# A decoder trunk kernel: the rotation's cosine product stays in PSUM, its sine halves and doubled keys are one operation each, and two softmax row tiles share one reciprocal

## The chip, the cores and the metric

The kernel runs on one core of a Trainium2 chip. The metric is the device time of one execution, in microseconds (us). The core's engines work side by side, each through its own queue of instructions in order: PE (TensorE, matrix products and transposes; its weight loads are shown as PEld), DVE (VectorE), ACT (ScalarE), POOL (GpSimd) and SP (which issues the DMAs). Semaphores hold an instruction back until what it needs is there. SBUF is the working memory, PSUM the memory into which PE writes, in banks of 512 f32 columns.

## The reference, cut to what matters

Two layers over 512 tokens of width 1024. Each layer is a mixer of three attention groups and then a gated MLP with a short convolution, both with norms before and after.

```
proj = h @ w_in                                  # one projection, cut into q, k, v of three head groups
rope(x): x1, x2 = x[..., :8], x[..., 8:16]       # HEAD_DIM 64, of which 16 are rotated
    concat([x1*cos - x2*sin, x2*cos + x1*sin, x[..., 16:]])
o_fox = fox_attention(q, k, v, log_f)            # 4 heads, not rotated
o_nsa = nsa_attention(rope(nq), rope(kc), vc, rope(ks), vs, rope(kw), vw, gates, ...)   # 8 heads, 2 key groups
o_dil = dilated_attention(rope(dq), rope(dk), dv)                                       # 4 heads
masked_softmax(s): e = exp(s - max(s)); e / sum(e)
x = x + rms_norm(concat(o_fox, o_nsa, o_dil) @ w_out)
x = x + rms_norm(conv_ffn(rms_norm(x)))
```

## The kernel before

**Numbers.** A matrix operand is held as a high part and a low part (hi and lo, `wh`/`wl`, `ph`/`pl`), and a product is three matmuls (hi·hi, hi·lo, lo·hi). For each such operand ACT copies the high part and DVE or POOL subtracts it from the original to get the low part. So every evacuation of PSUM and every arriving weight costs one ACT and one DVE or POOL operation.

**Attention stage.** `units` is a list of 96 softmax row tiles per layer: for each head (and for each of two branches in the nsa group) four tiles t = 0 to 3 of 128 queries, with 128·(t+1) keys. A loop runs over slots; in each slot every unit that is under way takes one step: scores (PE), `st_max` (DVE: mask and row minimum, since scores are negated), `st_exp` (ACT, with the row sum), `st_norm` (a reciprocal of the sum on DVE, then POOL scales the row, line 1133), `st_turn` (PE transposes, line 1146), `st_keep_hi` (ACT, line 1157) and `st_keep_lo` (DVE, line 1162), values (PE), `st_out`. `LAGS` says how many slots after its scores a unit takes each step: norm two slots, transposes four. The transposes of t = 0 are made together with those of t = 1.

**Between the units** the loop sprinkles pieces of the projections (`main_pieces`): `kc`, `ks`, `nq0`, `kw`, `nq1`, `dv`, `dq`, `dk`. A projection makes four token tiles s = 0 to 3 of 256 columns; tiles 0 and 1 lie in one PSUM bank, 2 and 3 in the next. Each tile is evacuated by `rope`: a cosine product `t1` (line 468) and two sine products into halves of `t2` (lines 469 and 470), all read from PSUM and written to SBUF tiles named `rope`; then for each destination an addition (line 472, `r<-rope,rope`) and an ACT copy of the 48 columns that are not rotated (line 473). Keys (`ks`, `kw`, `dk`) are stored twice side by side, so they have two destinations. Four token tiles are then transposed (line 737) and split into `k` or `q` (lines 493 and 486). In the same stretch the compressed branch builds windows `wt` (line 795), half on DVE, half on POOL.

**Order.** PE's order is written out by hand; the order on DVE, ACT and POOL is set by a scheduler that plans all instructions beforehand, and each engine then goes through its list.

Of the kernel before, what the change touches and what calls it, by code (L numbers as in the profile page):

```python
# [9 lines left out]
F32 = mybir.dt.float32  # L10
F32R = mybir.dt.float32r
I32 = mybir.dt.int32
AF = mybir.ActivationFunctionType
ALU = mybir.AluOpType
# [60 lines left out]
def tile_hybrid_block(  # L75
# [6 lines left out]
    nc = tc.nc  # L82
# [6 lines left out]
    small = ctx.enter_context(tc.tile_pool(name="small", bufs=8))  # L89
# [5 lines left out]
    def nm(p):  # L95
        uid[0] += 1
        return f"{p}_{uid[0]}"
# [7 lines left out]
    def rt(shape=(128, 512), dt=F32):  # L105
        return rowp.tile(list(shape), dt, tag="r", name=nm("r"))

    def st(n, tag="sm"):
        return small.tile([128, n], F32, tag=tag, name=nm("sm"))
# [7 lines left out]
    def bc(ap, axis, n):  # L117
        a = ap.unsqueeze(axis)
        shape = list(a.shape)
        shape[axis] = n  # L120
        return a.to_broadcast(shape)
# [318 lines left out]
    cc = const.tile([128, NST, 16], F32, name="cc")  # L440
    ss = const.tile([128, NST, 16], F32, name="ss")
# [6 lines left out]
    for l in range(DEPTH):  # L448
# [14 lines left out]
                mm(o, HL(k)[:, sl], w[0][:, i], False, last and z == n - 1)  # L463

        def rope(dst, src, s, nh):
            t1 = small.tile([128, nh, 16], F32, tag="rope", bufs=4, name=nm("rope"))
            t2 = small.tile([128, nh, 16], F32, tag="rope", bufs=4, name=nm("rope"))
            nc.vector.tensor_mul(t1, src[:, :, 0:16], bc(cc[:, s], 1, nh))
            nc.vector.tensor_mul(t2[:, :, 0:8], src[:, :, 8:16], bc(ss[:, s, 0:8], 1, nh))
            nc.vector.tensor_mul(t2[:, :, 8:16], src[:, :, 0:8], bc(ss[:, s, 8:16], 1, nh))  # L470
            for d in dst:
                nc.vector.tensor_add(d[:, :, 0:16], t1, t2)  # L472
                nc.scalar.activation(d[:, :, 16:64], src[:, :, 16:64], AF.Copy)

        def t_block(tiles, c0):
            p = ps("pt")
# [27 lines left out]
        def hd(ap):  # L504
            return ap.rearrange("p (h d) -> p h d", d=64)
# [5 lines left out]
        bias = small.tile([128, 28], F32, tag="gbias", bufs=1, name=nm("gbias"))  # L511
# [9 lines left out]
        for s in range(NST):  # L521
# [5 lines left out]
            p = ps("s")[:, 0:284]  # L527
# [6 lines left out]
            d = rt((128, 4, 2, 64))  # L534
# [7 lines left out]
        for j in range(3):  # L542
            d = crow[44 * (j % 2):44 * (j % 2) + 44, j // 2, :]
# [170 lines left out]
        def staged(key, turned, dup, nh, v=None, plain=0):  # L714

            tl = []

            def evac(s, p):
                w = nh * 64 * (2 if dup else 1)
                d = rt((128, w + plain))  # L720
                if dup:
                    e = d[:, 0:w].rearrange("p (h u d) -> p h u d", h=nh, u=2)
                    rope([e[:, :, 0, :], e[:, :, 1, :]], hd(p[:, 0:64 * nh]), s, nh)
                else:
                    rope([hd(d[:, 0:w])], hd(p[:, 0:64 * nh]), s, nh)
                if plain:
                    nc.scalar.activation(d[:, w:w + plain], p[:, 64 * nh:64 * nh + plain], AF.Copy)
                if v is not None:
                    if s == 0:
                        store[v] = new_v()  # L730
                    v_evac(store[v], s, p[:, 64 * nh:64 * nh + 128])
                tl.append(d)

            def turn(j):
                p = ps(TT)
                for s in range(NST):
                    nc.tensor.transpose(p[:, 128 * s:128 * s + 128], tl[s][:, 128 * j:128 * j + 128], ident)  # L737
                pieces.later(EV[3], keep, p)

            def keep(p):  # L740
                store.setdefault(key, []).append((k_evac if dup else q_evac)(p))

            return evac, [(turn, j) for j in range(nh * (2 if dup else 1) // 2)]
# [6 lines left out]
        def main_pieces():  # L750
# [2 lines left out]

            def kc_evac(s, p):
                d = rt((128, 256))
                rope([hd(d[:, 0:128])], hd(p[:, 0:128]), s, 2)
                nc.scalar.activation(d[:, 128:256], p[:, 128:256], AF.Copy)
                tl.append(d)

# [356 lines left out]

        def st_max(u):
            n = u["n"]
            row, sm_ = rt(), st(3, "sf")
            u["row"], u["sm"] = row, sm_  # L1120
            nc.vector.tensor_tensor_reduce(row[:, 0:n], u["S"][:, 0:n], u["mask"][:, 512 - n:512], op0=ALU.add,  # L1121
                                           op1=ALU.min, scale=1.0, scalar=3.0e38, accum_out=sm_[:, 0:1])

        def st_exp(u):
            n, row, sm_ = u["n"], u["row"], u["sm"]
            nc.scalar.activation(row[:, 0:n], row[:, 0:n], AF.Exp, scale=-1.0, bias=sm_[:, 0:1],  # L1126
                                 accum_out=sm_[:, 1:2])

        def st_norm(u):
            n, row, sm_ = u["n"], u["row"], u["sm"]  # L1130
            nc.vector.reciprocal(sm_[:, 2:3], sm_[:, 1:2])  # L1131
            g_ = 1.0 if u["gate"] is None else gates[:, u["t"], u["gate"]:u["gate"] + 1]
            nc.gpsimd.tensor_scalar(row[:, 0:n], row[:, 0:n], sm_[:, 2:3], g_, op0=ALU.mult, op1=ALU.mult)  # L1133

        def st_turn(u):
            if u["t"] == 0:
# [276 lines left out]
```

## Time and profile before

| what | value |
|---|---|
| time, median of 3 runs (lowest to highest) | 1375.59 us (1375.48 to 1377.04) |
| the profiled execution: its own time, and its span from first to last instruction | 1373.89 us, 1372.1 us |
| PE busy | 1337.1 us, 97% |
| DVE busy | 865.5 us, 63% |
| ACT busy | 730.7 us, 53% |
| POOL busy | 287.4 us, 21% |
| granted TensorE clock, share of full | 0.998 |

The first layer's attention stage lies at about 50 to 350 us of the span, its MLP at 350 to 690; the second layer's at 720 to 1030 and after. Busy shares over the whole span are means over these stages. In the views, `A<-B` names the tile written and the tiles read, `L472` is line 472 of the kernel, and "idle before <-X" says which instruction ended an engine's wait.

### The profile page before, as it was taken

The numbers are of one execution on the slowest core, as the hardware profiler recorded it, in microseconds if no ns is written. First come the engines' busy times: TensorE is split into PE (matmuls) and PEld (weight loads), VectorE is DVE, ScalarE is ACT, GpSimd is POOL, SyncE is SP. The second block draws the span as 40 slices with busy tenths as digits, with TensorE's granted clock in tenths as the row PEclk, the third lists the DMA queues.
The fourth block names the chain that finished last, engine by engine and source line by source line (L and its number), as shares of the span: only waits on it lengthen the run. The fifth ranks groups of instructions, "written<-read, shape, count | busy, mean of one in ns | idle before, by whom it ended". The sixth has DMA issues, their size and how long they took to land.

```text
span 1372.1 us, 21230 instructions
## 1 busy us (share of the span) xinstructions
PE 1337.1 (97%) x7855; PEld 1176.5 (86%) x7855; DVE 865.5 (63%) x2021; ACT 730.7 (53%) x1530; POOL 287.4 (21%) x343
## 2 busy tenths in 40 slices
PE   9999999999999999999999999999999999999997
PEld 8899998978888888888898899999798888888886
DVE  7688877778655555433464887877876555554334
ACT  6567767777533333333465677677774333333232
POOL 1364753341000000000004546633210000000000
PEclk9999999999999999999999999999999999999999
DMA  6323311141333333323333142012323333332231
GB/s 180 93 63 110 100 43 48 47 138 32 108 93 97 102 92 96 104 93 123 111 97 91 48 138 78 32 47 63 123 62 93 104 96 92 99 101 92 94 122 62
DMA packets 145520, 123.76 MB, mean 90 GB/s; under 512 B 8264, under 2 KB 135688, under 8 KB 145416
## 3 DMA queue, kind: packets, MB, share of 16 engines
q1 hardware_dynamic: 145416, 122.40, 29.4%
q8 instruction: 62, 1.02, 0.3%
q14 instruction: 42, 0.34, 0.1%
HBM read 118.19 MB, written 4.19 MB: 89 GB/s over the span
## 4 chain that ended last, share of the span: by engine, by line
PE 81%; DVE 10%; ACT 5%; issue 2%; POOL 1%; DMA 0%; SPq 0%; ACTq 0%; DVEq 0%
PE acc L115 36%; PE s L115 18%; PE pt L115 12%; PE o L115 10%; PE pt L1146 3%; DVE r L472 1%; DVE wt L795 1%; DVE hl L271 1%; DVE r L1121 1%; DVE pl L1162 1%; ACT r L1126 1%; PE pt L737 1%; ACT hh L270 1%; ACT r L1195 0%; ACT ph L1157 0%
## 5 line engine op out<-in xcount | busy, mean ns | idle before, releaser
L154 DVE TENSOR_TENSOR wl_up<-raw_up,wh_up 128x1024 fp32r<-128x1024 f32 x78 | 95.6, 1226 | 170.8 <-ACT wh_up L146 170.8
L146 ACT ACTIVATE wh_up<-raw_up 128x1024 fp32r<-128x1024 f32 (+1 forms) x90 | 89.6, 1001 | 160.4 <-PE acc L115 68.1
L154 DVE TENSOR_TENSOR wl_wd<-raw_wd,wh_wd 128x1024 fp32r<-128x1024 f32 x42 | 51.5, 1226 | 133.7 <-ACT wh_wd L146 133.7
L146 ACT ACTIVATE wh_wd<-raw_wd 128x1024 fp32r<-128x1024 f32 x42 | 44.5, 1060 | 144.8 <-PE pt L115 135.5
L1126 ACT ACTIVATE r<-r,sm 128x128 f32<-128x128 f32 x192 | 106.7, 557 | 22.1 <-DVE sm L1121 20.5
L1133 POOL TENSOR_SCALAR r<-r,sm,gates 128x128 f32<-128x128 f32 (+3 forms) x128 | 86.4, 680 | 117.0 <-DVE sm L1131 80.5
L115 PE MATMUL acc<-hl,wh_up 128*128 128x512 f32 (+1 forms) x272 | 102.4, 377 | 0.0
L115 PE MATMUL acc<-hh,wh_up 128*128 128x512 f32 (+1 forms) x272 | 102.4, 377 | 0.0
L115 PE MATMUL acc<-hh,wl_up 128*128 128x512 f32 (+1 forms) x272 | 102.4, 377 | 0.0
L150 POOL TENSOR_TENSOR wl_kc<-raw_kc,wh_kc 128x512 fp32r<-128x512 f32 x8 | 11.8, 1489 | 417.6 <-ACT wh_kc L146 416.7
L115 PE MATMUL s<-k,q 128*128 128x512 f32 (+3 forms) x384 | 96.4, 337 | 2.8 <-DVE sm L1121 1.3
L1162 DVE TENSOR_TENSOR pl<-pt,ph 128x384 fp32r<-128x384 f32 x144 | 85.5, 595 | 13.4 <-ACT ph L1157 11.6
L1121 DVE CUSTOM_DVE_ANT_0 r<-s,cmask 128x128 f32<-128x128 f32 (+3 forms) x160 | 75.8, 483 | 18.9 <-PE s L115 13.5
L1157 ACT ACTIVATE ph<-pt 128x384 fp32r<-128x384 f32 x144 | 75.5, 524 | 21.6 <-PE pt L1146 20.0
L1146 PE MATMUL pt<-ident,r 128*128 128x128 f32 x480 | 77.2, 275 | 7.2 <-DVE pl L1162 5.7
L115 PE MATMUL acc<-wh_wd,gh 128*128 128x512 f32 x252 | 83.7, 389 | 0.0
L115 PE MATMUL s<-hh,wh_up 128*128 128x512 f32 (+1 forms) x224 | 80.4, 359 | 0.0
L115 PE MATMUL s<-hl,wh_up 128*128 128x512 f32 (+1 forms) x224 | 80.4, 359 | 0.0
L115 PE MATMUL s<-hh,wl_up 128*128 128x512 f32 (+1 forms) x224 | 80.4, 359 | 0.0
L1337 ACT ACTIVATE r<-r 128x512 f32<-128x512 f32 x44 | 27.8, 633 | 85.7 <-DVE r L1318 85.5
L1146 PEld LDWEIGHTS pt<-ident,r 128*128 128x128 f32 x480 | 55.2, 140 | 16.2 <-POOL r L1133 7.1
L115 PE MATMUL acc<-wh_wo,mix 128*128 128x256 f32 (+1 forms) x296 | 67.6, 305 | 0.0
(440 smaller groups left out, 4145.6 us busy)
## 6 DMA issues: line engine op xcount, KB each, us to landing
raw_up<-in_w_up_dram SPq DMA_DIRECT2D x88, 512.0 KB, 3.8
raw_wd<-in_w_down_dram SPq DMA_DIRECT2D x44, 512.0 KB, 3.4
raw_wo<-in_w_out_dram SPq DMA_DIRECT2D x16, 512.0 KB, 3.5
x<-in_x_dram SPq DMA_DIRECT2D x8, 512.0 KB, 5.9
raw_nq<-in_w_in_dram SPq DMA_DIRECT2D x8, 512.0 KB, 3.5
raw_w<-in_cmp_w_k_dram SPq DMA_DIRECT2D x8, 512.0 KB, 3.9
raw_w<-in_cmp_w_v_dram SPq DMA_DIRECT2D x8, 512.0 KB, 3.8
raw_fk<-in_w_in_dram SPq DMA_DIRECT2D x4, 512.0 KB, 5.6
```

The source lines that it names most:

```text
L115: nc.tensor.matmul(o, lhsT=lhsT, rhs=rhs, start=start, stop=stop, skip_group_check=True)
L146: nc.scalar.activation(hi[:, ks], raw[:, ks], AF.Copy)
L154: nc.vector.tensor_sub(lo[:, ks], raw[:, ks], f(hi)[:, ks])
L270: nc.scalar.activation(hi, src, AF.Copy, scale=gain[:, k:k + 1])
L271: nc.vector.scalar_tensor_tensor(lo, src, gain[:, k:k + 1], f(hi), op0=ALU.mult, op1=ALU.subtract)
L1121: nc.vector.tensor_tensor_reduce(row[:, 0:n], u["S"][:, 0:n], u["mask"][:, 512 - n:512], op0=ALU.add, op1=ALU.min, scale=1.0, scalar=3.0e3 ...
L1126: nc.scalar.activation(row[:, 0:n], row[:, 0:n], AF.Exp, scale=-1.0, bias=sm_[:, 0:1], accum_out=sm_[:, 1:2])
L1133: nc.gpsimd.tensor_scalar(row[:, 0:n], row[:, 0:n], sm_[:, 2:3], g_, op0=ALU.mult, op1=ALU.mult)
L1146: nc.tensor.transpose(p[:, 128 * c:128 * c + 128], blocks[z], ident)
L1157: nc.scalar.activation(hi, src, AF.Copy)
L1162: nc.vector.tensor_sub(*u["lo"])
L1337: nc.scalar.activation(cd[0], cd[0], AF.Silu)
```

## The change

`rope` now takes one destination with a dimension u for the copies. It makes `t2` in one operation, reading the two halves of the rotated columns in swapped order (a step of -8). The cosine product is written over the 16 columns in PSUM from which it is read. One addition, with `t1` from PSUM and `t2` from SBUF, both broadcast over u, writes all copies; one ACT copy does the same for the other 48 columns. In the softmax, the row sums of t = 0 and t = 1 lie in two columns of one small tile; the step of t = 0 only remembers its unit, and the step of t = 1 makes one reciprocal of both columns and then has POOL scale both rows. t = 2 and t = 3 keep their own reciprocals.

```diff
         def rope(dst, src, s, nh):
-            t1 = small.tile([128, nh, 16], F32, tag="rope", bufs=4, name=nm("rope"))
+
+            t1 = src[:, :, 0:16]
             t2 = small.tile([128, nh, 16], F32, tag="rope", bufs=4, name=nm("rope"))
-            nc.vector.tensor_mul(t1, src[:, :, 0:16], bc(cc[:, s], 1, nh))
-            nc.vector.tensor_mul(t2[:, :, 0:8], src[:, :, 8:16], bc(ss[:, s, 0:8], 1, nh))
-            nc.vector.tensor_mul(t2[:, :, 8:16], src[:, :, 0:8], bc(ss[:, s, 8:16], 1, nh))
-            for d in dst:
-                nc.vector.tensor_add(d[:, :, 0:16], t1, t2)
-                nc.scalar.activation(d[:, :, 16:64], src[:, :, 16:64], AF.Copy)
+            z = src[:, :, 8:16]
+            swapped = bass.AP(tensor=z.tensor, offset=z.offset, ap=[list(z.ap[0]), list(z.ap[1]), [-8, 2], [1, 8]])
+            nc.vector.tensor_mul(t2.rearrange("p h (i d) -> p h i d", i=2), swapped,
+                                 bc(ss[:, s].rearrange("p (i d) -> p i d", i=2), 1, nh))
+            nc.vector.tensor_mul(t1, t1, bc(cc[:, s], 1, nh))
+
+            nu = dst.shape[2]
+            nc.vector.tensor_add(dst[:, :, :, 0:16], bc(t1, 2, nu), bc(t2, 2, nu))
+            nc.scalar.activation(dst[:, :, :, 16:64], bc(src[:, :, 16:64], 2, nu), AF.Copy)
...
         def st_max(u):
             n = u["n"]
-            row, sm_ = rt(), st(3, "sf")
-            u["row"], u["sm"] = row, sm_
+            t = u["t"]
+            row = u["row"] = rt()
+            if t != 1:
+                state["m"] = st(4 if t == 0 else 2, "sf")
+            n2 = 2 if t < 2 else 1
+            u["sm"] = sm_ = [st(1, "mn")] + [state["m"][:, n2 * i + t % n2:n2 * i + t % n2 + 1] for i in range(2)]
+            u["all"] = [state["m"][:, n2 * i:n2 * i + n2] for i in range(2)]
...
         def st_norm(u):
-            n, row, sm_ = u["n"], u["row"], u["sm"]
-            nc.vector.reciprocal(sm_[:, 2:3], sm_[:, 1:2])
-            g_ = 1.0 if u["gate"] is None else gates[:, u["t"], u["gate"]:u["gate"] + 1]
-            nc.gpsimd.tensor_scalar(row[:, 0:n], row[:, 0:n], sm_[:, 2:3], g_, op0=ALU.mult, op1=ALU.mult)
+
+            if u["t"] == 0:
+                state["u"] = u
+                return
+            nc.vector.reciprocal(u["all"][1], u["all"][0])
+            for z in (state["u"], u) if u["t"] == 1 else (u,):
+                n, row = z["n"], z["row"]
+                g_ = 1.0 if z["gate"] is None else gates[:, z["t"], z["gate"]:z["gate"] + 1]
+                nc.gpsimd.tensor_scalar(row[:, 0:n], row[:, 0:n], z["sm"][2], g_, op0=ALU.mult, op1=ALU.mult)
```

PE and SP go through the same instructions in the same order as before. On the other three engines the scheduler has planned anew.

First place: DVE, in the first layer, where the last two token tiles of the `ks` projection (`acc_961` before, `acc_954` now) are evacuated while the windows `wt` are built; L1121 and L1126 are the row minimum of a softmax tile, L502 and L506 the low part of the values. Before:

```order
L472 TENSOR_TENSOR r_1204<-rope_1205,rope_1206 128x2x16 x2
L1121 ISA r_1221,sm_1222<-s_1140,cmask 128x512
L1121 ISA sm_1222 128x1
L795 TENSOR_TENSOR wt_1201<-r_1199,posT_803 64x16x31
L502 TENSOR_TENSOR v_1137<-acc_961,v_1137 128x2x64
L468 TENSOR_TENSOR rope_1254<-acc_961,cc 128x32
L469 TENSOR_TENSOR rope_1255<-acc_961,ss 128x2x8
L470 TENSOR_TENSOR rope_1255<-acc_961,ss 128x2x8
L795 TENSOR_TENSOR wt_1201<-r_1199,posT_803 64x16x31
L472 TENSOR_TENSOR r_1253<-rope_1254,rope_1255 128x2x16 x2
```

And with the change:

```order
L476 TENSOR_TENSOR r_1191<-acc_954,rope_1192 128x4x16
L1126 ISA r_1204,sm_1206<-s_1129,cmask 128x512
L1126 ISA sm_1206 128x1
L795 TENSOR_TENSOR wt_1188<-r_1186,posT_803 64x16x31
L506 TENSOR_TENSOR v_1126<-acc_954,v_1126 128x2x64
L471 TENSOR_TENSOR rope_1238<-acc_954,ss 128x32
L795 TENSOR_TENSOR wt_1188<-r_1186,posT_803 64x16x31
L473 TENSOR_TENSOR acc_954<-acc_954,cc 128x2x16
L1139 RECIPROCAL sm_1205<-sm_1205 128x1
L476 TENSOR_TENSOR r_1237<-acc_954,rope_1238 128x4x16
```

The sequence around the windows is the same; each pair of additions of two SBUF tiles is one addition with one operand in PSUM, and a reciprocal now stands ahead of the second addition.

Second place: POOL, in the first layer's first two softmax heads (L1133 and L1143 scale a row; L150 is a weight's low part). Before:

```order
L1133 TENSOR_SCALAR r_1017<-r_1017,sm_1018 128x512
L1133 TENSOR_SCALAR r_1044<-r_1044,sm_1045 128x128
L150 TENSOR_TENSOR wl_nq_1_203_1233<-raw_nq_1_170_1075,wh_nq_1_202_1232 128x512
L795 TENSOR_TENSOR wt_1073<-r_1071,posT_803 64x16x31 x2
L150 TENSOR_TENSOR wl_nq_1_203_1233<-raw_nq_1_170_1075,wh_nq_1_202_1232 128x512
L1133 TENSOR_SCALAR r_1103<-r_1103,sm_1104 128x256
```

And with the change:

```order
L1143 TENSOR_SCALAR r_1010<-r_1010,sm_1011 128x512
L150 TENSOR_TENSOR wl_nq_1_202_1217<-raw_nq_1_170_1070,wh_nq_1_201_1216 128x512
L795 TENSOR_TENSOR wt_1068<-r_1066,posT_803 64x16x31 x2
L150 TENSOR_TENSOR wl_nq_1_202_1217<-raw_nq_1_170_1070,wh_nq_1_201_1216 128x512
L1143 TENSOR_SCALAR r_1038<-r_1038,sm_1039 128x128
L1143 TENSOR_SCALAR r_1098<-r_1098,sm_1039 128x256
```

The row of t = 0 (128x128) is scaled just ahead of the row of t = 1 (128x256) and no longer before the weight and window work.

## Rows read from the trace of the kernel before

**Rows 1.** The page, part 1: busy us of each engine (share) and instructions.
```profile
PE 1337.1 (97%) x7855; PEld 1176.5 (86%) x7855; DVE 865.5 (63%) x2021; ACT 730.7 (53%) x1530; POOL 287.4 (21%) x343
```

**Rows 2.** Stretches: attention, then MLP; busy us of each engine, clock, DMA share, GB/s.
```profile
50.00:100.00 50.00, 47.95 (x378) 45.73 (x377) 34.57 (x105) 27.91 (x80) 31.16 (x29) 1.00 0.23 65
400.00:450.00 50.00, 50.00 (x222) 41.40 (x221) 27.54 (x33) 18.70 (x23) 0.00 (x0) 1.00 0.33 95
```

**Rows 3.** PE's waits: us in total, times, longest.
```profile
PE pt L1146 <- DVE pl L1162: 5.7, 6, 1.8
PE pt L737 <- DVE pl L1162: 4.6, 4, 2.2
```

**Rows 4.** PE's timeline where it waits: start, us, what, idle time before it.
```profile
93.00 0.55 PE L737 MATMUL pt<-ident,r 128*128 128x128 f32 x3 [1.45 <-DVE pl L1162]
...
132.49 0.50 PE L115 MATMUL s<-k,q 128*128 128x128 f32 x2 [0.48 <-DVE k L493]
...
765.47 0.44 PE L115 MATMUL s<-k,q 128*128 128x384 f32 x1 [0.68 <-DVE sm L1121]
...
771.43 0.44 PE L737 MATMUL pt<-ident,r 128*128 128x128 f32 x2 [2.17 <-DVE pl L1162]
```

**Rows 5.** DVE's timeline, 84.5 to 93 us.
```profile
84.70 0.16 DVE L469 TENSOR_TENSOR rope<-acc,ss 128x16 f32<-128x16 f32 x1
84.79 0.16 DVE L470 TENSOR_TENSOR rope<-acc,ss 128x16 f32<-128x16 f32 x1
85.05 1.39 DVE L472 TENSOR_TENSOR r<-rope,rope 128x32 f32<-128x32 f32 x2
...
88.95 1.45 DVE L795 TENSOR_TENSOR wt<-r,posT 64x496 f32<-64x496 f32 x1
90.42 1.24 DVE L472 TENSOR_TENSOR r<-rope,rope 128x32 f32<-128x32 f32 x2
```

**Rows 6.** POOL's timeline, same stretch.
```profile
85.11 1.29 POOL L802 TENSOR_TENSOR wth<-wt,wth 128x512 fp32r<-128x512 f32 x1
...
87.73 3.78 POOL L795 TENSOR_TENSOR wt<-r,posT 64x496 f32<-64x496 f32 x2
```

**Rows 7.** The tile `rope`: shortest/median/longest ns, first and last start.
```profile
L472 DVE TENSOR_TENSOR r<-rope,rope x80: 176/215/1331, 64.4 to 913.7; 128x32 f32<-128x32 f32 x40, 128x64 f32<-128x64 f32 x40
L468 DVE TENSOR_TENSOR rope<-acc,cc x56: 169/204/225, 64.0 to 911.3; 128x64 f32<-128x64 f32 x32, 128x32 f32<-128x32 f32 x24
```

**Rows 8.** DVE's groups by shape: count, busy us, mean ns, idle before.
```profile
L1131 DVE RECIPROCAL sm<-sm 128x1 f32<-128x1 f32 x192 | 29.3, 155 | 17.2 <-ACT r L1126 16.5
...
L472 DVE TENSOR_TENSOR r<-rope,rope 128x32 f32<-128x32 f32 x40 | 16.1, 434 | 1.1
...
L472 DVE TENSOR_TENSOR r<-rope,rope 128x64 f32<-128x64 f32 x40 | 12.5, 328 | 0.8
```

**Rows 9.** DVE's timeline in the second layer, same place as rows 5.
```profile
762.25 2.56 DVE L472 TENSOR_TENSOR r<-rope,rope 128x32 f32<-128x32 f32 x2
...
768.87 1.22 DVE L472 TENSOR_TENSOR r<-rope,rope 128x32 f32<-128x32 f32 x2
```

**Rows 10.** Timelines at the `kw` projection, first layer: DVE, then ACT.
```profile
124.07 2.58 DVE L472 TENSOR_TENSOR r<-rope,rope 128x32 f32<-128x32 f32 x2
...
130.57 0.60 ACT L492 ACTIVATE k<-pt 128x512 fp32r<-128x512 f32 x1 [0.40 <-PE pt L737]
```

**Rows 11.** All engines' waits: us in total, times, longest.
```profile
ACT r L473 <- DVE rope L470: 21.8, 18, 2.6
...
PEld pt L1146 <- POOL r L1133: 7.1, 8, 2.0
```

**Rows 12.** What ended DVE's idle time before line 468: us, times.
```profile
  ACT r L473: 0.5, 2
```

**Rows 13.** ACT's and POOL's groups by shape: count, busy us, mean ns, idle before.
```profile
L473 ACT ACTIVATE r<-acc 128x192 f32<-128x192 f32 x40 | 12.2, 326 | 8.3 <-DVE rope L470 5.6 <-PE pt L1146 2.6
...
L1133 POOL TENSOR_SCALAR r<-r,sm,gates 128x128 f32<-128x128 f32 x32 | 15.2, 476 | 24.5 <-DVE sm L1131 19.4 <-PE s L115 3.5 <-DVE rope L468 1.6
```

More of the change, by code (lines that the diff above doesn't have):

```diff
@@ L720, in evac @@
                 d = rt((128, w + plain))
[L721 to L725, printed above, removed]
+                rope(d[:, 0:w].rearrange("p (h u d) -> p h u d", h=nh, d=64), hd(p[:, 0:64 * nh]), s, nh)
                 if plain:
@@ L755, in kc_evac @@
                 d = rt((128, 256))
-                rope([hd(d[:, 0:128])], hd(p[:, 0:128]), s, 2)
+                rope(d[:, 0:128].rearrange("p (h u d) -> p h u d", h=2, d=64), hd(p[:, 0:128]), s, 2)
                 nc.scalar.activation(d[:, 128:256], p[:, 128:256], AF.Copy)
@@ L1118, in st_max @@
             n = u["n"]
-            row, sm_ = rt(), st(3, "sf")
-            u["row"], u["sm"] = row, sm_
+            t = u["t"]
[5 more added lines that the diff above has]
+            u["all"] = [state["m"][:, n2 * i:n2 * i + n2] for i in range(2)]
             nc.vector.tensor_tensor_reduce(row[:, 0:n], u["S"][:, 0:n], u["mask"][:, 512 - n:512], op0=ALU.add,
-                                           op1=ALU.min, scale=1.0, scalar=3.0e38, accum_out=sm_[:, 0:1])
+                                           op1=ALU.min, scale=1.0, scalar=3.0e38, accum_out=sm_[0])
         def st_exp(u):
             n, row, sm_ = u["n"], u["row"], u["sm"]
-            nc.scalar.activation(row[:, 0:n], row[:, 0:n], AF.Exp, scale=-1.0, bias=sm_[:, 0:1],
-                                 accum_out=sm_[:, 1:2])
+            nc.scalar.activation(row[:, 0:n], row[:, 0:n], AF.Exp, scale=-1.0, bias=sm_[0],
+                                 accum_out=sm_[1])
         def st_norm(u):
-            n, row, sm_ = u["n"], u["row"], u["sm"]
-            nc.vector.reciprocal(sm_[:, 2:3], sm_[:, 1:2])
-            g_ = 1.0 if u["gate"] is None else gates[:, u["t"], u["gate"]:u["gate"] + 1]
-            nc.gpsimd.tensor_scalar(row[:, 0:n], row[:, 0:n], sm_[:, 2:3], g_, op0=ALU.mult, op1=ALU.mult)
+            if u["t"] == 0:
[6 more added lines that the diff above has]
+                nc.gpsimd.tensor_scalar(row[:, 0:n], row[:, 0:n], z["sm"][2], g_, op0=ALU.mult, op1=ALU.mult)
         def st_turn(u):
```

## The prediction

> **What bounds the kernel.** I read the busy times first. PE is busy for 1337.1 us of a span of 1372.1, DVE for 63% of it [rows 1]. So 35 us at most are to be had without taking work from PE, and this change takes none. Then the table by stretches: in the MLP PE is busy for all 50.00 of 50 us, in the attention stage for 47.95, with DVE at 34.57 there [rows 2]. Everything that the change touches lies in the attention stages, so its worth is what it does to the few microseconds that PE waits there. Third, PE's waits by releaser: the longest entries are waits for DVE, 5.7 and 4.6 us, both ended by line 1162, the low part of the turned softmax rows [rows 3]. That line is cheap and regular; it is late because of what stands ahead of it in DVE's queue. So last I went to PE's gaps one by one and read DVE's timeline backwards from each.
>
> Four gaps have rotations ahead of them: 1.45 us at 93.00 and, at the same place in the second layer, 0.68 at 765.47 and 2.17 at 771.43; and 0.48 at 132.49 [rows 4], with its twin in the second layer, which I take as equal. In the first, the addition pair at 85.05 takes 1.39 us and the pair at 90.42 takes 1.24 [rows 5], where an addition has a median of 0.215 and reaches 1.331 [rows 7]. POOL's operation at 85.11 ends at 86.40, and the pair ends at 86.44; POOL's two at 87.73 end at 91.51, the pair at 91.66 [rows 5, 6]. So the additions stand still until POOL is through. The cosine product, which reads one operand from PSUM and one from SBUF, never takes over 0.225 in 56 times, though it runs in the same stretches [rows 7]. What tells them apart in these rows is the two SBUF operands of line 472.
>
> **The change part by part.**
>
> *The additions.* Their 80 take 16.1 + 12.5 = 28.6 us [rows 8]; at 0.2 each they would take 16, so 12.6 us are standing still. After the change 56 are left, with one operand in PSUM. No row shows such an addition, nor DVE writing PSUM, which the cosine product now does. The nearest rows are line 468 (0.204) and the free line 472 (0.215) [rows 7]; I take 0.2 for each, and as the other end twice that, which over 112 operations would be 22 us more on DVE.
>
> [...]
>
> *Place A, windows and `ks`.* First layer: the pair at 85.05 becomes one addition of 0.2, so DVE is 1.2 us earlier, and the one at 90.42 is 1.0 earlier by itself. In between stand two window operations with two SBUF operands (1.45 at 88.95 [rows 5]), which also meet POOL, so part of the first 1.2 may be lost there. The gap of 1.45 needs 1.45 of the 2.2: I take 1.3 (bounds 0 and 1.45). Second layer: the pairs take 2.56 and 1.22 [rows 9] and would take 0.25 each, 3.3 us less, against gaps of 0.68 + 2.17 = 2.85; by the same share I take 2.4 (bounds 0.95, if only the last addition counts, and 2.85).
>
> *Place B, `kw`.* The pair at 124.07 takes 2.58 [rows 10] and DVE then works on until the gap at 132.49. 2.3 us earlier is more than the gap needs, but the low part of `k` for which PE waits also needs ACT's copy, 130.57 to 131.17 [rows 10], which itself waits for PE's transposes. 0.45 of 0.48 in each layer, 0.9 (bounds 0 and 0.96).
>
> *Fewer operations.* 48 of 192 reciprocals go, 0.155 each, 7.4 us of DVE [rows 8], and 56 sine products, which in a row cost only 0.09 each (84.70 to 84.79 [rows 5]), 5 us. These lie across both attention stages, where PE is waiting for some 4% of the time [rows 2], so most of it shortens nothing: 0.5 (bounds 0 and 3).
>
> *What it adds to `rope`.* Before, the three products do not depend on each other, and only the addition waits: 84.79 to 85.05, 0.26 [rows 5]. Now the cosine product overwrites columns that the sine product reads, so it waits for that, and the addition waits for it: two steps of 0.27 and 0.2, about 0.75, against 0.1 + 0.09 + 0.26 + 0.2 = 0.65. 0.1 us for each of 56 tiles is 5.6 us of DVE, which cancels the saved sine products. ACT's copy, which already waits for line 470 (21.8 us in 18 waits [rows 11]), now waits for the addition, some 0.4 later; what stands behind it in ACT's queue is a copy of values or a softmax copy. DVE's first product of the next tile in the bank waits for ACT's copy: that wait is there today and costs 0.5 us in two waits [rows 12]. I charge 0.4 (bounds 0 and the rival below).
>
> *Rows of t = 0 scaled later.* POOL scales the row of t = 0 just ahead of that of t = 1, 0.476 [rows 13]. The transposes come two slots after, so there is usually cover; PE's weight loads already wait for POOL 8 times, 7.1 us in all [rows 11]. If each of those became 0.476 longer, it would be 3.8; in the tail of each stage the two stand together already. I charge 0.3 (bounds 0 and 3.8).
>
> **The sum.** 1.3 + 2.4 + 0.9 + 0.5 - 0.4 - 0.3 = 4.4 us. Against the profiled execution's own 1373.89 (span 1372.1 and 1.8 around it) that is 1369.5; that execution was 1.7 below the median of the three timed runs, 1375.59, to which I refer the forecast: 1371.2. A difference under 0.2%, 2.75 us, can hardly be told from none here, so the forecast stands 1.65 us beyond that bound.
>
> **Rivals.**
>
> *The standing still moves on* (15%). The next operation with two SBUF operands meets the POOL operation in place of the addition: at place A the window operations of line 795 stand right behind the first addition. Then only the last addition of the place counts, 0.95 in each layer, and with B, the fewer operations and the costs the gain is 1.9 + 0.9 + 0.5 - 0.7 = 2.6: 1373.0. For it: 1.45 for a window operation beside POOL [rows 5]. Against it: at B the operations behind the pair are rotations and value splits that read PSUM.
>
> [...]
>
> *The serial rotation ends slower* (14%). In 28 of the 56 tiles DVE's sine product waits for ACT's copy of the tile before it in its bank, and everything behind it on DVE, the row minima and line 1162, waits too. If the copy (0.326 for 192 columns [rows 13]), now 0.4 later, is waited for in full at each, that is 28 x 0.73 = 20 us of DVE standing still, more than the 12.6 gained. PE then waits longer at the projections' ends instead of shorter; at a quarter of the surplus and with the gaps of A and B as they were, and the transposes behind POOL's paired rows, I reckon 3 us more than before: 1378.5. It decides from a mean wait of 0.45 us per tile pair (12.6/28). Against it: the scheduler has put other work between most of these pairs, and the waits of today are 0.5 us in all [rows 12].
>
> *The write into PSUM is dear* (8%). At the upper bound, 22 us of DVE eat the 12.6 + 7.4: no change, 1375.3.
>
> *A lighter DVE helps everywhere* (13%). The other gaps behind line 1162 [rows 3] shrink as well, the fewer operations reach their bound of 3, and A and B close fully (1.45 + 2.85 + 0.96 = 5.3): some 8 us, 1367.
>
> **How the numbers follow.** The forecast case has 50% (1368.5 to 1373.2, nine in ten of it beyond the bound). Faster by over 0.2%: 0.45 + 0.13 + a third of the first rival, 0.63. Within 0.2%: 0.05 + 0.10 + 0.08, 0.23. Slower: 0.14. The range leaves out the far ends of the last and of the slower rival: 1366.5 to 1377.0.
>
> **What the profile after would show.** Right: no rotation's addition over 0.3 us, their busy time near 12 us in place of 28.6; PE's gaps at about 93, 132 and 765 to 771 gone or under 0.4; PE's busy time unchanged, its idle time some 4 us less; DVE busy about 30 us less. The first rival would show window operations longer by what the additions lost. The slower one would show DVE waiting for the ACT copy of the rotation by more than 10 us, and PE waiting for DVE at the turns of `q` and `k`. What would make me wrong altogether is a new plan that moves line 1162 behind other work at places where today it is on time, since each such case costs PE 1 to 2 us and I read the order only where the gaps are today.

## The result, and the profile of the changed kernel

The changed kernel takes 1368.51 us (median of 6 executions, 1368.02 to 1369.85) against 1375.61 for the kernel before (6 executions beside them): a ratio of 0.9947, 95% interval 0.9934 to 0.9960. It is 7.1 us faster; the forecast was 4.4. The profiled execution took 1369.85 (span 1367.9) and is the slowest of its six, while that of before was 1.7 under its median; so the two spans differ by 4.2 only, and the rest of this document has to say where the other 3 us lie.

The page's part 1, as [rows 1]:

```profile
PE 1338.0 (98%) x7855; PEld 1177.9 (86%) x7855; DVE 850.4 (62%) x1893; ACT 728.2 (53%) x1506; POOL 287.0 (21%) x343
```

The rotation's lines, as [rows 7, 8] (here over all shapes: busy us, mean ns, idle before). Line 471 is the sine product, 473 the cosine product written into PSUM, 476 the addition; line 1139 is the reciprocal.

```profile
L1139 DVE RECIPROCAL sm<-sm 128x2 f32<-128x2 f32 x144 | 22.7, 158 | 17.6 <-ACT r L1131 17.1
...
L795 DVE TENSOR_TENSOR wt<-r,posT 64x496 f32<-64x496 f32 x8 | 13.9, 1740 | 2.5 <-ACT r L783 2.4
L476 DVE TENSOR_TENSOR r<-acc,rope 128x64 f32<-128x64 f32 (+2 forms) x56 | 12.6, 226 | 1.9
L473 DVE TENSOR_TENSOR acc<-acc,cc 128x64 f32<-128x64 f32 (+1 forms) x56 | 12.0, 215 | 1.4
```

No addition stands still any more: in the view by tile they take 190 to 293 ns. Writing PSUM costs hardly more than writing SBUF did (215 ns a cosine product, 203 before).

PE's timeline at place A in both layers, as [rows 4]:

```profile
92.37 0.66 PE L737 MATMUL pt<-ident,r 128*128 128x128 f32 x4 [0.55 <-DVE pl L1172]
766.99 0.66 PE L737 MATMUL pt<-ident,r 128*128 128x128 f32 x4 [0.55 <-DVE pl L1172]
```

Line 1172 is what line 1162 was. The gap of 1.45 is 0.55, those of 0.68 and 2.17 are one of 0.55, and at place B (0.48 at 132.49) there is none. The stretch of both places, first layer, before and after (busy us of PE, PEld, DVE, ACT, POOL, then clock, DMA share, GB/s):

```profile
60.00:150.00 90.00, 87.77 (x699) 85.20 (x698) 68.91 (x228) 61.43 (x170) 48.66 (x50) 1.00 0.31 89
```

```profile
60.00:150.00 90.00, 89.42 (x712) 86.86 (x711) 65.31 (x197) 61.51 (x165) 49.03 (x51) 1.00 0.31 90
```

PE's idle time there goes from 2.23 to 0.58 us. What is left at A reads in DVE's timeline, as [rows 5]:

```profile
86.53 1.81 DVE L795 TENSOR_TENSOR wt<-r,posT 64x496 f32<-64x496 f32 x1
...
88.66 1.59 DVE L795 TENSOR_TENSOR wt<-r,posT 64x496 f32<-64x496 f32 x1
...
91.42 0.42 DVE L1126 CUSTOM_DVE_ANT_0 r<-s,cmask 128x256 f32<-128x256 f32 x1 [0.51 <-POOL wt L795]
```

Before, the first of the two was (the second is in [rows 5]):

```profile
86.98 1.48 DVE L795 TENSOR_TENSOR wt<-r,posT 64x496 f32<-64x496 f32 x1
```

The window additions, which keep two SBUF operands, now take 1.81 and 1.59 where they took 1.48 and 1.45: some of the standing still has moved on to them. And a row minimum behind them now waits itself.

**The clock.** Elsewhere PE's waits are the same within 0.3 us, with one exception that is not a wait. PE, second layer, in single microseconds (clock is the third number from the end):

```profile
893.00:894.00 1.00, 0.68 (x5) 0.47 (x4) 0.97 (x3) 0.00 (x0) 0.00 (x0) 1.00 0.00 0
894.00:895.00 1.00, 0.80 (x4) 0.83 (x5) 0.61 (x5) 0.91 (x3) 0.20 (x1) 0.51 0.48 143
895.00:896.00 1.00, 1.00 (x7) 1.00 (x6) 0.25 (x1) 0.98 (x5) 1.00 (x1) 0.50 0.82 324
896.00:897.00 1.00, 1.00 (x6) 1.00 (x6) 0.97 (x3) 0.98 (x4) 0.09 (x1) 0.50 0.14 57
897.00:898.00 1.00, 1.00 (x6) 0.98 (x6) 0.79 (x3) 0.20 (x1) 0.80 (x2) 0.79 0.00 0
```

At the last of three gaps (0.47, 0.17 and 0.53 us at 891 to 894) the granted clock falls to 0.50 and stays there for some 3 us, with PE busy from 894.20 on. Matmuls of 256 columns start 0.213 us apart in it (895.08 to 897.22), so PE goes through 1.2 columns a ns; before the gaps, at 1.00, they start 0.12 apart (889.76 to 890.49). The first trace of before has the same three gaps (0.47, 0.18 and 0.52 at 896 to 900) and no such fall. By the table below the fall costs 1.4 us, and the profiled execution is 1.3 above its median; the other five have no trace.

**A table of stretches.** PE's order is the same in every kernel here, so the start of the same matmul can be read from each PE timeline, and the time between two of them compared. us; * marks a stretch in which the trace shows the clock at 0.50 for some 3 us. "55 to 162" holds place A and B of the first layer, "720 to 836" those of the second; the times are those of the changed kernel. The kernels below it are those of the experiments.

| kernel | start to 55 | 55 to 162 | 162 to 217 | 217 to 720 | 720 to 836 | 836 to 891 | 891 to end | median us |
|---|---|---|---|---|---|---|---|---|
| before, [rows 1 to 13] | 54.8 | 108.4 | 55.5 | 504.1 | 118.9 | 55.3 | 475.2 | 1375.6 |
| changed | 55.0 | 106.7 | 55.0 | 504.1 | 115.5 | 54.9 | 476.6* | 1368.51 |
| e1 rotation alone | 55.7 | 106.6 | 56.9* | 504.3 | 115.5 | 56.9* | 476.7* | 1373.62 |
| e2 reciprocal alone | 55.2 | 108.2 | 55.4 | 504.1 | 116.9 | 55.2 | 475.2 | 1375.02 |
| e3 merged, SBUF | 55.0 | 107.2 | 55.1 | 504.1 | 116.0 | 55.1 | 475.2 | 1369.32 |
| e4 PSUM, not merged | 55.0 | 109.0 | 55.6 | 505.9* | 117.9 | 55.6 | 475.5 | 1375.77 |
| e5 before again | 55.8 | 108.4 | 55.4 | 504.1 | 120.0* | 55.4 | 475.2 | 1376.40 |
| e6 as e3, reciprocal shared | 54.6 | 107.3 | 55.1 | 504.1 | 116.1 | 55.2 | 475.2 | 1369.65 |
| e7 sine halves alone | 54.9 | 108.8 | 55.2 | 504.1 | 116.5 | 55.2 | 475.2 | 1372.84 |
| e8 doubled keys alone | 55.8 | 106.7 | 55.1 | 504.1 | 116.6 | 55.2 | 475.2 | 1370.04 |
| e9 as e1, line 950 on ACT | 54.9 | 106.6 | 54.2 | 504.0 | 115.6 | 54.2 | 475.2 | 1366.77 |
| e10 changed, line 952 split | 54.6 | 106.7 | 54.5 | 504.1 | 115.6 | 54.5 | 476.7* | 1367.73 |
| e11 windows on DVE | 54.9 | 110.5 | 54.9 | 505.8* | 120.1* | 54.9 | 475.2 | 1377.90 |
| e12 changed, line 950 on ACT | 54.8 | 106.7 | 54.2 | 504.1 | 115.5 | 54.2 | 475.2 | 1366.73 |

A stretch with a fall is longer than the same one without: by 1.4 and 1.5 us at the end (476.6 and 476.7 against 475.2), by 1.7 and 1.8 at 217 to 720 (505.8 and 505.9 against 504.1), and by 1.1 between the two executions of before (120.0 against 118.9). The start differs by up to 1.2 us between these executions. The traces of e2 and e7 are those of their fastest executions (1371.94 and 1371.54), so their stretches add up to less than their medians. The change itself is worth 1.7 + 0.5 + 3.4 + 0.4 = 6.0 us between the two first rows, most of it in the two stretches with A and B.

### The profile page after: what moved, and what is told of

Read it like the earlier page. It is cut to its first block, busy times and chain, and to the rows that moved or that the text cites. A ratio compares the mean times of both kernels' runs of the same rounds, so it can differ in the third digit from the quotient of the medians.

```text
span 1367.9 us, 21028 instructions
## 1 busy us (share of the span) xinstructions
PE 1338.0 (98%) x7855; PEld 1177.9 (86%) x7855; DVE 850.4 (62%) x1893; ACT 728.2 (53%) x1506; POOL 287.0 (21%) x343
## 4 chain that ended last, share of the span: by engine, by line
PE 85%; DVE 7%; ACT 4%; POOL 2%; issue 2%; DMA 0%; SPq 0%; ACTq 0%; POOLq 0%; DVEq 0%
PE acc L115 39%; PE s L115 19%; PE pt L115 13%; PE o L115 10%; PE pt L1156 3%; POOL wt L795 1%; PE pt L737 1%; DVE hl L271 1%; DVE pl L1172 1%; DVE r L1126 1%; ACT r L1131 1%; DVE x L913 0%; ACT hh L270 0%; ACT h L310 0%; ACT ph L1167 0%
## 5 line engine op out<-in xcount | busy, mean ns | idle before, releaser
L1143 POOL TENSOR_SCALAR r<-r,sm,gates 128x128 f32<-128x128 f32 (+3 forms) x128 | 86.4, 683 | 126.1 <-DVE sm L1139 82.3
L1131 ACT ACTIVATE r<-r,sm 128x128 f32<-128x128 f32 x192 | 106.7, 557 | 9.3 <-DVE sm L1126 8.4
L150 POOL TENSOR_TENSOR wl_kc<-raw_kc,wh_kc 128x512 fp32r<-128x512 f32 x8 | 11.8, 1490 | 417.6 <-ACT wh_kc L146 416.8
L1126 DVE CUSTOM_DVE_ANT_0 r<-s,cmask 128x128 f32<-128x128 f32 (+3 forms) x160 | 76.0, 482 | 20.6 <-PE s L115 16.2
L1156 PEld LDWEIGHTS pt<-ident,r 128*128 128x128 f32 x480 | 55.4, 141 | 15.9 <-POOL r L1143 6.8
```

The source lines that it names most:

```text
L1143: nc.gpsimd.tensor_scalar(row[:, 0:n], row[:, 0:n], z["sm"][2], g_, op0=ALU.mult, op1=ALU.mult)
L1156: nc.tensor.transpose(p[:, 128 * c:128 * c + 128], blocks[z], ident)
```

## The experiments

### e1_rope_only and e2_pair_only: each half of the change

e1 has the new `rope` and the softmax steps of before; e2 the old `rope` and the shared reciprocal.

> The new rotation alone, softmax tiles with their own reciprocals as before. Theory of the lock (the additions with two SBUF operands no longer stand still behind POOL, and that ends PE's gaps at places A and B): nearly the whole gain, 1368.5 to 1370.5 us, PE's idle time 4 to 5 us less than before, the gap at 93 near 0.5. Rival 'fewer operations' (a lighter DVE wherever PE waits): about two thirds of the gain, 1370.5 to 1372, since a third of the removed DVE operations are reciprocals. Rival 'the shared reciprocal is what counts': 1374 to 1376.

> The shared reciprocal alone, the rotation as before. Theory of the lock: 1374.5 to 1376, gaps at 93, 132 and 765 to 771 as before, the rotation's additions still up to 1.3 us. Rival 'fewer operations': 1372.5 to 1374. Rival 'the shared reciprocal is what counts': 1369 to 1371.

Measured: e1 1373.62, ratio 0.9978 (0.9968 to 0.9988); e2 1375.02, 0.9992 (0.9983 to 1.0001). Neither half gives the gain, and no one theory had both: e2 is where the standing still had it, but e1 is 3 us slower than that theory allowed, though its additions run free and its gap near 93 is 0.55. The table says where: at A and B e1 gains all that the changed kernel gains (106.6, 115.5). It loses at 162 to 217 and at 836 to 891. DVE's and POOL's timelines there, then PE's and the clock:

```profile
162.24 0.72 DVE L950 TENSOR_SCALAR r<-r 128x256 f32<-128x256 f32 x1
```

```profile
162.07 0.74 POOL L947 TENSOR_TENSOR r<-w2r,r 128x256 fp32r<-128x256 f32 x1
```

```profile
167.32 0.52 PE L1146 MATMUL pt<-ident,r 128*128 128x128 f32 x3 [1.94 <-DVE pl L1162]
```

```profile
168.00:172.00 4.00, 4.00 (x19) 3.81 (x18) 1.49 (x9) 1.36 (x5) 3.37 (x5) 0.57 0.44 131
```

Line 950 (an addition of 1 in the compressed branch) takes 0.72 next to POOL's line 947, in the second layer 0.71; in before, the changed kernel, e3 and e5 it takes 0.29 to 0.30. DVE works without a pause from there to line 1162, so PE's gap is 1.94 where the changed kernel has 1.52, and behind it the clock falls. Most of what e1 loses is the clock: its one execution with a mean clock of 0.999 took 1369.02. So far this was read, not tried; e9 tries it.

### e3_merged_sbuf and e4_psum_only: merging against standing still

e3 merges the operations but keeps the cosine product in SBUF, so that its additions still have two SBUF operands; e4 keeps it in PSUM, with two sine products, two additions and two copies. Both have the softmax of before.

```diff
 e3
-            t1 = src[:, :, 0:16]
+            t1 = small.tile([128, nh, 16], F32, tag="rope", bufs=4, name=nm("rope"))
 e4 (against before)
-            t1 = small.tile([128, nh, 16], F32, tag="rope", bufs=4, name=nm("rope"))
+            t1 = src[:, :, 0:16]
```

> One sine product, one addition and one copy for doubled keys, as in the change, but the cosine product goes to an SBUF tile, so the addition keeps two SBUF operands; softmax as before. Theory of the lock: the additions that are left still stand behind POOL, up to 1.3 us each, and the time is 1372.5 to 1375.5 (a little better than before, since two additions that each waited for one POOL operation are one). Rival 'fewer operations': 1370 to 1372, as good as the rotation of the change.

> The cosine product stays in PSUM, but there are two sine products, an addition and a copy for each destination as before; softmax as before. Theory of the lock: no addition over 0.3 us, their busy time near 17 us in place of 28.6, time 1369 to 1371.5. Rival 'fewer operations': 1374.5 to 1376.5, since not one operation is saved and the products now wait for each other.

Measured: e3 1369.32, ratio 0.9952 (0.9939 to 0.9964); e4 1375.77, 1.0005 (0.9995 to 1.0014). Neither lies in the range of the theory of the lock; the rival, that the number of operations counts, was within a microsecond on both. Merging alone gives nearly the whole gain, and the product in PSUM alone gives none. The additions of e3, then of e4 (shortest, median, longest ns):

```profile
L476 DVE TENSOR_TENSOR r<-rope,rope x56: 192/238/1169, 64.5 to 907.9; 128x64 f32<-128x64 f32 x40, 128x32 f32<-128x32 f32 x8, 128x128 f32<-128x128 f32 x8
```

```profile
L472 DVE TENSOR_TENSOR r<-acc,rope x80: 173/196/226, 64.8 to 917.6; 128x32 f32<-128x32 f32 x40, 128x64 f32<-128x64 f32 x40
```

So two SBUF operands are what makes these additions stand still (1.17 us at the longest in e3, 0.23 in e4), as forecast. But e3 does not leave the standing still as it was: where a pair of additions stood, one is left. At B it takes 0.23 us where the pair took 2.58 [rows 10], and at A, in the first layer, the two left take 2.11 where the two pairs took 2.63 [rows 5]; in the second layer it is 2.10 against 3.78 [rows 9]. DVE's timeline of e3 at A, first layer:

```profile
85.14 0.94 DVE L476 TENSOR_TENSOR r<-rope,rope 128x64 f32<-128x64 f32 x1
...
90.02 1.17 DVE L476 TENSOR_TENSOR r<-rope,rope 128x64 f32<-128x64 f32 x1
```

And in e4 the gap behind the low part at A is gone in both layers (0.00 in place of 1.45 and of 0.68 + 2.17), as forecast, but other waits take its place. PE's timeline of e4, at A and at B:

```profile
93.03 0.33 PE L737 MATMUL pt<-ident,r 128*128 128x128 f32 x1 [0.90 <-ACT r L473]
...
128.14 0.36 PE L115 MATMUL acc<-wh_nq,hh 128*128 128x256 f32 x1 [0.85 <-DVE r L472]
```

PE no longer waits for the softmax row but for the rotation itself: at A for a copy, at B, before it writes `acc`, for an addition, which now reads PSUM. DVE's and ACT's timelines of e4 at A:

```profile
91.42 0.19 DVE L472 TENSOR_TENSOR r<-acc,rope 128x32 f32<-128x32 f32 x1
...
92.08 0.18 DVE L472 TENSOR_TENSOR r<-acc,rope 128x32 f32<-128x32 f32 x1
```

```profile
91.65 0.25 ACT L473 ACTIVATE r<-acc 128x96 f32<-128x96 f32 x1 [3.33 <-DVE r L472]
...
92.75 0.23 ACT L473 ACTIVATE r<-acc 128x96 f32<-128x96 f32 x1
```

Addition and copy alternate for the two destinations, and two row minima stand ahead of the second addition. All engines' waits show longer waits for the copies too, of e4 and then of the changed kernel; before, they waited 21.8 us in 18 waits, for the sine product [rows 11]:

```profile
ACT r L473 <- DVE r L472: 35.1, 30, 3.3
```

```profile
ACT r L477 <- DVE r L476: 28.6, 22, 3.0
```

With one addition and one copy the string has two links less. How much of e4's loss is the longer string, and how much the new plan of the scheduler, is not separated: PE also waits 0.85 us at 208.52 and at 887.90 for line 1047, a low part of the compressed branch, where before it waits 0.04.

### e7_sine_only and e8_dup_only: which merging

Both keep the cosine product in SBUF and the softmax of before. e7 has one sine product, but two additions and copies for doubled keys; e8 has two sine products, and one addition and one copy.

> Of the merged operations the sine halves alone: one sine product, two additions and two copies for doubled keys, cosine product in SBUF. If the number of rotation operations counts wherever they are taken away: 1372 to 1373.5. If only the additions and copies of the doubled keys count (they stand still behind POOL and make the ACT copies late): 1374.5 to 1376.5, gaps near 93 us at 1.45, 132 us at 0.3 to 0.5 and 771 us at 2.

> Of the merged operations the doubled keys alone: one addition and one copy write both copies, two sine products, cosine product in SBUF. If the doubled keys count: 1369.3 to 1371, gaps near 93 and 770 us at 0.8 and the one near 132 us gone. If the number of rotation operations counts wherever it is: 1371.5 to 1373.

Measured: e7 1372.84, ratio 0.9979 (0.9971 to 0.9988); e8 1370.04, 0.9961 (0.9947 to 0.9975). e8 came out where the doubled keys had it and e7 where the number of operations had it: the doubled keys alone give most, and the sine halves something too. The parts are not additive: against [rows 4] e7 is worse in the first layer and better in the second. PE's timeline of e7 at A, first and second layer, then of e8, second layer (it has no gap in the first):

```profile
93.95 0.66 PE L739 MATMUL pt<-ident,r 128*128 128x128 f32 x4 [2.19 <-DVE pl L1164]
769.62 0.66 PE L739 MATMUL pt<-ident,r 128*128 128x128 f32 x4 [0.98 <-DVE pl L1164]
```

```profile
768.57 0.66 PE L735 MATMUL pt<-ident,r 128*128 128x128 f32 x4 [1.25 <-DVE pl L1160]
```

The two layers do the same work there, and yet the gaps run from none to 2.19 us. DVE's timelines tell why: the additions, which [rows 5, 6] show standing until POOL's operation ends, take 0.23 to 2.15 us there. The additions at A in e7, then in e8, first and second layer:

```profile
85.17 2.15 DVE L474 TENSOR_TENSOR r<-rope,rope 128x32 f32<-128x32 f32 x2
...
91.41 1.21 DVE L474 TENSOR_TENSOR r<-rope,rope 128x32 f32<-128x32 f32 x2
...
762.12 1.00 DVE L474 TENSOR_TENSOR r<-rope,rope 128x32 f32<-128x32 f32 x2
...
767.04 1.24 DVE L474 TENSOR_TENSOR r<-rope,rope 128x32 f32<-128x32 f32 x2
```

```profile
85.96 0.23 DVE L474 TENSOR_TENSOR r<-rope,rope 128x64 f32<-128x64 f32 x1
...
90.09 1.17 DVE L474 TENSOR_TENSOR r<-rope,rope 128x64 f32<-128x64 f32 x1
...
760.78 1.35 DVE L474 TENSOR_TENSOR r<-rope,rope 128x64 f32<-128x64 f32 x1
...
766.07 1.17 DVE L474 TENSOR_TENSOR r<-rope,rope 128x64 f32<-128x64 f32 x1
```

The same sums for the kernels whose additions have two SBUF operands, beside PE's gap at A, us (e5 is the kernel before, and agrees with it within 0.02):

| kernel | first layer: additions | gap | second layer: additions | gap |
|---|---|---|---|---|
| e8 | 0.23 + 1.17 = 1.40 | 0.03 | 1.35 + 1.17 = 2.52 | 1.25 |
| e3 | 0.94 + 1.17 = 2.11 | 0.79 | 0.94 + 1.16 = 2.10 | 0.76 |
| e6 | 0.94 + 1.17 = 2.11 | 0.86 | 0.94 + 1.16 = 2.10 | 0.86 |
| e7 | 2.15 + 1.21 = 3.36 | 2.19 | 1.00 + 1.24 = 2.24 | 0.98 |
| e2 | 1.40 + 1.24 = 2.64 | 1.45 | 1.40 + 1.24 = 2.64 | 1.49 |
| before | 1.39 + 1.24 = 2.63 | 1.45 | 2.56 + 1.22 = 3.78 | 0.68 + 2.17 = 2.85 |

So at A the time of the additions sets the gap, as the prediction had it. The gaps of 0.8 that e8's expectation named came out as 0.03 and 1.25 for this reason.

### e5_before_again and e6_merged_sbuf_pair

> The kernel before, unchanged, for the trace of one more execution. Theory of the clock: executions of one kernel differ because TensorE's granted clock falls to half (0.50, 1.2 GHz) for some 3 us behind one or another of PE's gaps near 168, 222, 846 and 898 us, 1.6 us each, so an execution near 1376.7 has two such falls, PE busy near 1340.3 (1337.1 in the first trace, with none) and the same idle time between its matmuls, 26.4 us. Rival: the slower executions wait longer, so PE busy stays at 1337 and the idle time is 29 to 30 us.

> The merged operations with the cosine product in SBUF, and the shared reciprocal. If merging is what counts and the two others add nothing: 1368.8 to 1369.8, as with the merged operations alone. If the shared reciprocal adds something: 1367.5 to 1368.5. If the addition's operand in PSUM is needed beside the merging (standing still): over 1369.8, with the gap near 92 us still 0.8.

e5 measured 1376.40, ratio 1.0003 (0.9995 to 1.0012). Its profiled execution took 1375.90, and its trace has one fall, not two, and not at one of the four places named but at place A of the second layer, behind the gap of 2.17 that also the first trace has:

```profile
771.00:772.00 1.00, 0.00 (x0) 0.00 (x0) 1.00 (x8) 0.48 (x3) 0.25 (x1) 1.00 0.04 3
...
774.00:775.00 1.00, 1.00 (x7) 1.00 (x6) 0.68 (x3) 1.00 (x4) 0.46 (x1) 0.50 0.04 13
```

PE busy is 1338.4 (1337.1 in the first trace); the other microsecond went at the start (55.8 against 54.8). So of the two theories the clock is right for half of the difference, the start has the other half.

e6 measured 1369.65, ratio 0.9958 (0.9945 to 0.9970), and its gaps at A are 0.86. That is e3 again: the shared reciprocal adds nothing, and the operand in PSUM is worth something beside the merging. In the table the changed kernel is 0.6 + 0.1 + 0.6 + 0.3 = 1.6 us ahead of e6. By the times alone the two are not told apart, since the intervals of their ratios overlap, and e6's time lies where its expectation had "the two others add nothing"; the worth of the operand in PSUM rests on the table and on the gaps at A (0.55 against 0.86).

### e9_rope_only_one_on_act, e12_change_one_on_act and e10_split_recip

e9 is e1, and e12 the changed kernel, with one line on another engine; e10 is the changed kernel with the two reciprocals behind it a slot apart.

```diff
 e9, e12
-            nc.vector.tensor_scalar(t2, t2, 1.0, None, op0=ALU.add)          # line 950
+            nc.scalar.activation(t2, t2, AF.Copy, bias=1.0)
 e10
             for c in range(2):
                 nc.vector.reciprocal(t2[:, 128 * c:128 * c + 128], t2[:, 128 * c:128 * c + 128])   # line 952
-            yield
+                yield
             nc.gpsimd.tensor_mul(xc, xc, t2)
             yield
-            yield
```

> The new rotation with separate reciprocals, and the addition of line 950 (0.72 there, standing still behind POOL, 0.29 elsewhere) done by ACT. Theory: the rotation alone loses what the changed kernel has only because line 950 falls on a POOL operation at 162 and 839 us, which makes the gaps near 167 and 844 us 1.94 in place of 1.52 and brings the clock's fall behind them. Then the gaps are 1.6 at most, the falls there are gone, and the time is 1368.5 to 1370.5. Rival: the shared reciprocal is needed by itself for the rest of the gain: 1372.5 to 1374, as with the rotation alone.

> The changed kernel with the two reciprocals of line 952 (1.76 together, ahead of line 1172 at the gaps near 166 and 841 us) taken one slot apart. If the gaps there, 1.5 us each, are made by that work standing together: they fall to 0.6 to 0.9, and the time is 1366.3 to 1367.8. Rival: what is made up there comes back, since the product behind the reciprocals and the transposes of the compressed keys come later: 1368 to 1370.

> The changed kernel, shared reciprocal included, with the addition of line 950 done by ACT. If the shared reciprocal is worth nothing by itself: 1366.3 to 1367.3, the same as the new rotation with separate reciprocals and this edit (1366.8), with gaps near 165 and 839 us of 0.8. If it is worth its 48 operations somewhere: under 1366.3. If it costs, since the row of t = 0 is scaled later: over 1367.3, with PE's waits for the scaled rows longer than 6.8 us.

Measured: e9 1366.77, ratio 0.9930 (0.9918 to 0.9942); e12 1366.73, 0.9934 (0.9920 to 0.9948); e10 1367.73, 0.9939 (0.9927 to 0.9952). PE's timeline of e9 and of e10 where e1 had 1.94 and the changed kernel has 1.52:

```profile
165.44 0.52 PE L1146 MATMUL pt<-ident,r 128*128 128x128 f32 x3 [0.81 <-DVE q L490]
```

```profile
165.45 0.52 PE L1155 MATMUL pt<-ident,r 128*128 128x128 f32 x3 [1.08 <-POOL r L954]
```

With line 950 off DVE, e1 becomes 6.9 us faster, more than expected: the gap falls to 0.81, and no fall of the clock stands behind it. It falls to 0.81 in e12 too, where the line had taken only 0.30, so more than the line's standing still is in this, and the new plan may have a part. In e10 the reciprocals hold nothing up, but PE then waits for POOL's product behind them (line 954), so it gets only part of this, as its time within the expected bounds and its gap above them say. So what e1 lacked was not the shared reciprocal. e9 and e12 differ in that alone and take the same time: the shared reciprocal by itself is worth nothing. In the changed kernel it helped by accident: POOL's rows came at another moment, and line 947 starts 0.60 us ahead of line 950 (161.01 and 161.61) where in e1 it starts 0.17 ahead. e12 and e9 beat both kernels; by the table e12 is 1.5 us ahead of the changed kernel (0.8 + 0.7) without counting the clock.

### e11_windows_on_dve

```diff
-                WENG[gq].tensor_add(wt[64 * u:64 * u + 64, :, gq, 0:31], src,     # line 795
+                nc.vector.tensor_add(wt[64 * u:64 * u + 64, :, gq, 0:31], src,
```

> The changed kernel with all four window additions of line 795 on DVE and none on POOL. If the two engines' additions stand still behind each other (1.6 to 1.9 on each side, where an addition of 512 columns takes 0.68 on DVE when POOL is idle): four on DVE take 0.7 each, 2.8 in place of 3.4, the gaps near 92 and 767 us (0.55) shrink or stay, and the time is 1367.2 to 1368.8. Rival: a window addition takes 1.4 by itself, DVE gets 2 us more at each window, the gaps grow to 1.5 to 2.5, and the time is 1370 to 1372.

Measured: 1377.90, ratio 1.0007 (0.9999 to 1.0016): the whole gain is gone. The additions, and PE's timeline at A:

```profile
L795 DVE TENSOR_TENSOR wt<-r,posT x16: 975/1296/1898, 76.9 to 775.3; 64x496 f32<-64x496 f32 x16
```

```profile
95.28 0.66 PE L737 MATMUL pt<-ident,r 128*128 128x128 f32 x4 [2.74 <-DVE pl L1172]
98.10 0.66 PE L737 MATMUL pt<-ident,r 128*128 128x128 f32 x4 [0.74 <-DVE pl L1172]
```

With none on POOL, a window addition on DVE takes 0.98 at its shortest and 1.30 in the median, not 0.7. My price was the wrong one, and the rival's closer, though its time was 6 us too low. As an estimate from the shortest, DVE gets 2.0 us more at each window (two of 1.0); there are two windows in a layer, and the stretch with place A grows by 3.8 (110.5 against 106.7): by this estimate, what is added to DVE there reaches PE almost in full.

## Why the prediction was right, and where it was not

**The total** lay in the range and on the right side, 2.7 us above the forecast gain. Place A gave 0.9 in the first layer (forecast 1.3) and 2.3 in the second (2.4); place B 1.0 (0.9). Two gaps of 0.30 at 113 and 792 us also went, which I had not read, and 0.9 came from 162 to 217 and 836 to 891, against 0.5 for "fewer operations"; what brought it was not tried. Nothing shows of the 0.4 charged for the serial rotation nor of the 0.3 for the later rows of t = 0: PE's weight loads wait 6.8 us for POOL, 7.1 before. These make 5.7 of the table's 6.0, in place of 4.4. The rest is the clock, of which the prediction says nothing: of 87 executions of before the 10 with a mean clock of 0.999 took 1373.8 (median), 49 at 0.997 took 1376.4; of the changed kernel's six, three at 0.999 took 1368.1. At equal clock the gain is 5.7, and the other 1.4 goes with the changed kernel running more often at the full clock; that this came on the side of the forecast is luck. That before's slower executions have their falls where e5 has one is inferred from their mean clocks; only e5's trace shows one.

**What held.** The additions stand still behind POOL for the reason given (1.33 us at the longest with two SBUF operands, 0.29 with one), and the change ends it (12.6 us of busy time where I said 12). At A the time that they take sets PE's gap (the table under e7 and e8), and without it the gap behind the low part is gone (e4). At B this is weaker: in e7 no addition stands still there and 0.25 us is left.

**The step that failed** is how the sum was laid on the edits. It gave A and B to the additions' operand in PSUM, charged 0.4 for the rotation that this makes serial, and did not ask what merging gives without it. By itself that edit is worth nothing: the waits it brings, 0.90 at A and 0.85 at B (e4), take back what the gap at A gives. Merging by itself gives 4.4 us at equal clock (e3 1369.3 against 1373.8; 6.4 by the medians), since a pair that could stand still twice (2.58 at the longest [rows 10]) is one addition that can stand still once (1.17, e3). Beside the merging the operand in PSUM is worth 1.6 (e6 against the changed kernel), and the serial rotation's price does not show. The sum was right for the places and wrong in its parts, and since the three edits came together, the total could not show it.

**The rivals.** That the standing still moves on to line 795 is true and small: those eight operations take 13.9 us, 13.1 before. That the serial rotation ends slower is true without the merging: in e4 it cancels what the additions gain. In the changed kernel DVE waits 0.9 us for the copies, far from the 10 named. That PSUM is dear to write fell (215 ns). That a lighter DVE helps everywhere is at most half true: 0.9 us outside A and B.

**What I said the profile would show:** additions under 0.3 us, right (0.293); gaps gone at 132, right, but 0.55 left at A where I said under 0.4; PE's idle time down by 4, it was 5.1, from 26.4 to 21.3 between its matmuls. DVE's busy time down by 30 was wrong: it fell by 15.1. The groups' own sums fell by 29.6 (the rotation's lines and the reciprocals, 88.4 to 58.8), but short operations overlap in the records, each 0.16 long and 0.09 behind the last [rows 5], and the page counts time in which any runs; the window additions also take 0.8 more. I had added up durations and compared them with a total that doesn't.

## What to carry to other kernels

Where one engine is the bound, look for the operation that it waits for and count the whole string of work on the other engines that leads to it: a repair that lengthens the string (an in-place product with two additions and two copies behind it) can take back what it gives. Try each edit of a change alone and each left out: here one of three was worth nothing, one nothing by itself and 1.6 us beside another, and one most of the gain. Then look in the trace whether an experiment left alone what it was meant to leave alone: e3 kept both SBUF operands, and its additions stood still less all the same. Before saying that two kernels differ, compare their traces by the same instruction's start, and take the clock's falls and the start out.

## What the runs showed of the hardware that I had not expected

- The granted clock falls from 1.00 to 0.50 for some 3 us shortly behind gaps of PE: behind 1.94 in e1, behind 2.17 in e5, behind 2.75 in e11 (772 to 776), and at the last of three gaps of 0.17 to 0.53 in a row in the changed kernel. It comes in some executions and not in others with the same gaps (2.17 in both traces of before, one fall), so a gap costs its own length and, in some executions, 1.1 to 1.8 us more (the table of stretches).
- A DVE operation with one SBUF operand can stand still behind POOL as well: line 950 takes 0.72 and 0.71 in e1, where it starts 0.17 behind POOL's line 947 (162.24 and 162.07, 838.97 and 838.80), and 0.29 to 0.30 in before, the changed kernel, e3 and e5. The prediction looked only at operations with two SBUF operands.
- Next to POOL's window additions, those on DVE take 1.43 to 1.90 us (before and the changed kernel); with none on POOL 0.98 at the shortest and 1.30 in the median (e11).
